# SwiGLU mixer of a two-layer diffusion trunk: plain block products for four tiles per half at both ends, norm by quarters, VectorE sums, stores issued by ScalarE

## The chip, the cores and the metric

The kernel runs on one core of a Trainium2 chip. The metric is the time of one execution on the device in microseconds (us), the median of several runs. The engines are named as in the profile: PE (TensorE, matmuls), PEld (its weight loads), DVE (VectorE), ACT (ScalarE), POOL (GpSimd), and SP, which only issues DMA. Each engine works its instructions in order, so a DMA that waits for its data holds up whatever stands behind it on the engine that issues it.

## The reference

One step of a trunk of two layers on 1152 tokens (1024 of a sample, 128 of a prompt) of width 1024, in fp32. `ada_mod` makes six modulation vectors per layer from `silu(c) @ w_ada` (1024 by 6144).

```python
for l in range(DEPTH):                      # l = 0: attention and retention, l = 1: gMLP
    h = modulate(rmsnorm(x, norm_g[l, 0]), sh1, sc1)
    y = ab(h) if l % 2 == 0 else chunk_gmlp(h)     # both end in an output projection
    x = x + g1 * y
    h = modulate(rmsnorm(x, norm_g[l, 1]), sh2, sc2)
    x = x + g2 * swiglu(h)
y = rmsnorm(x, final_norm_g)

def swiglu(h):                               # the mixer: d = 1024, D_FF = 2816
    return (silu(h @ w_gate) * (h @ w_up)) @ w_down
def chunk_gmlp(h):
    u, v = split(gelu(h @ w_in)); v = layernorm(v)
    v = einsum('gij,bnjgd->bnigd', w_s, chunks(v)) + b_s
    return (u * v) @ w_out
```

## The kernel before, in words

Tokens lie along the free axis, in two halves c = 0, 1 of 576, each of two pieces h = 0, 1 of 288; a quarter is one (c, h). X, the residual stream, lies in tiles x0 to x3 (`xp(f, c, h)` is one 128x288 block of it). An fp32 product is three matmuls on operands split in a high and a low part (hi by hi, hi by lo, lo by hi): ACT copies the high part, another engine subtracts it for the low one. That is the "prep" of an operand.

The **mixer** (`class Mixer`, `run`) works through `UNITS`, one unit for each 128 rows of D_FF (22 in all): the unit's gate and up products for one half or both. Then it does the `GROUPS` of down products. Both use seven block products in Strassen's manner in place of eight (`gate_up`, `down`, `steps`, `product`): 7 x 4 x 3 = 84 matmuls 128x288 for a unit and a half. Their seven left operands are built from the weight blocks by 4 sums, 7 copies and 7 subtractions 128x512 (`prep`), and their seven right operands (`RIGHT`, in tiles hq, h and x) from the normalised X. Units 20 and 21 are done for c = 0 alone at the start and for c = 1 alone at the end; the 20 others take both halves. After two units `combine` makes the seven right operands of the down product from their outputs (7 sums, 7 copies, 7 low parts, on DVE, POOL and ACT), and stores high and low part in DRAM (`hcd`). Before the downs `hload` brings them back, and X comes back from its spill `xtd`.

`proj_out` is the output projection ahead of a mixer: matmuls, `resid` adds into X, `squares` sums the squares, then `rnorm` scales a half of X, first c = 0, later c = 1, and builds the right operands, on DVE and POOL by turns. `xnorm` does the first norm of layer 1, behind the downs of layer 0. `last0`, `last1` and `done` take up the squares behind the last downs and finish.

Weights come as a **stream** `W` in program order: DMAs of 512 KB issued by SP into three slots of a staging tile ST, consumed by preps into rings w0 to w4. The ada weights of layer 1 are in that stream too, as 24 pairs of DMAs and 8 matmuls each (`in_w_ada`), one pair behind nearly every unit of mixer 0. Background generators (`bg`, `bg2`) fill the gaps; a planner decides only where in the program order their steps stand. All instructions are recorded by one helper, so that every row of the profile says L129.

## Time and profile before

| | |
|---|---|
| median of 3 runs | 2997.62 us (2991.59 to 2999.55) |
| profiled execution | 3002.7 us, its span 3000.9 us |
| PE busy | 2730.0 us (91%), 18667 matmuls |
| DVE, ACT, POOL busy | 1734.2, 1181.9, 1075.3 us |
| mean granted PE clock | 0.954 of full speed |

The span is the time from the first instruction to the last; the profiled execution took 1.8 us more than it. The stages are: attention layer to 825 us, output projection and entry of mixer 0 to 975, its units to about 1500, its end to 1600, its downs to 1725, then the hand-over to the gMLP layer, the gMLP layer to 2100, the entry of mixer 1 to 2225, its units to 2650, its end to 2775, downs and final norm to 3001.

### The profile page before, as it was taken

How to read it: one execution, taken by the hardware profiler on the slowest of the kernel's cores; microseconds unless marked ns; L12 is line 12 of the kernel's file. 1: busy time of each engine (PE TensorE's matmuls, PEld its weight loads, DVE VectorE, ACT ScalarE, POOL GpSimd, SP SyncE). 2: the span in 40 equal slices, each digit the busy share in tenths (PEclk: the TensorE clock that was granted, in tenths of full speed). 3: DMA queues.
4: the chain of work that ended last, by engine and by line, in shares of the span. 5: the costliest groups of instructions: out<-in, count | busy, mean ns of one | idle time of the engine just before them, and what ended most of it. 6: DMA issues, size and time to landing. Idle time of an engine off the chain costs nothing. (4 is left out here: it accounts for less than half of the span.)

```text
span 3000.9 us, 48879 instructions
## 1 busy us (share of the span) xinstructions
PE 2730.0 (91%) x18667; PEld 2570.7 (86%) x18667; DVE 1734.2 (58%) x3212; ACT 1181.9 (39%) x2385; POOL 1075.3 (36%) x978
## 2 busy tenths in 40 slices
PE   6999998998978899899789979999879999989996
PEld 5887897888977788888779977899879999988995
DVE  5651336877465444554577864534675555458875
ACT  5542225776344333333322244223554343342224
POOL 1120014665054232332366562000534334346553
PEclk8999998999988999899899999999989999999997
DMA  9385435332423554354598624124215344469761
GB/s 285 100 275 168 134 95 151 79 79 66 148 77 102 163 182 140 131 176 140 184 312 259 215 80 133 29 61 127 81 56 167 110 141 141 132 225 300 253 200 64
DMA packets 429344, 447.16 MB, mean 149 GB/s; under 512 B 25579, under 2 KB 368374, under 8 KB 427574
## 3 DMA queue, kind: packets, MB, share of 16 engines
q1 hardware_dynamic: 426704, 441.20, 46.3%
q8 instruction: 147, 2.41, 0.3%
q10 hardware_dynamic: 2406, 2.85, 0.3%
q14 instruction: 87, 0.71, 0.1%
HBM read 302.03 MB, written 141.93 MB: 148 GB/s over the span
## 5 line engine op out<-in xcount | busy, mean ns | idle before, releaser
L129 PE MATMUL PS<-hq,w 128*128 128x288 f32 (+1 forms) x10080 | 1521.7, 308 | 151.1 <-ACT SC L129 73.0
L129 PEld LDWEIGHTS PS<-hq,w 128*128 128x128 f32 x10080 | 1453.6, 194 | 186.3 <-ACT SC L129 86.0
L129 ACT CAST w<-ST 128x512 fp32r<-128x512 f32 (+3 forms) x733 | 377.5, 545 | 563.4 <-POOL ST L129 296.0
L129 DVE TENSOR_TENSOR w<-ST,w 128x512 fp32r<-128x512 f32 (+3 forms) x551 | 456.0, 849 | 240.5 <-ACT w L129 237.7
L129 DVE SCALAR_TENSOR_TENSOR x<-PS,mod,x 128x288 f32<-128x288 f32 (+2 forms) x944 | 388.4, 445 | 152.6 <-PE PS L129 147.0
L129 PE MATMUL PS<-h,w 128*128 128x288 f32 (+1 forms) x2702 | 418.9, 303 | 44.7 <-DVE x L129 25.0
L129 PEld LDWEIGHTS PS<-h,w 128*128 128x128 f32 (+1 forms) x2702 | 380.8, 192 | 74.3 <-DVE x L129 30.6
L129 POOL TENSOR_TENSOR SC<-SC 128x288 f32<-128x288 f32 (+2 forms) x122 | 116.9, 972 | 491.6 <-ACT SC L129 472.7
L129 PE MATMUL PS<-x,w 128*128 128x288 f32 (+1 forms) x1728 | 269.4, 304 | 12.8 <-ACT x L129 6.6
L129 PEld LDWEIGHTS PS<-x,w 128*128 128x128 f32 x1728 | 248.1, 192 | 19.5 <-ACT x L129 8.3
L129 ACT COPY SC<-PS 128x576 f32<-128x576 f32 (+8 forms) x249 | 128.6, 518 | 326.8 <-PE PS L129 304.7
L129 DVE TENSOR_TENSOR SC<-PS,SC 128x576 f32<-128x576 f32 (+3 forms) x131 | 90.3, 690 | 223.9 <-PE PS L129 216.1
L129 POOL TENSOR_TENSOR SC<-SC,x 128x576 fp32r<-128x576 f32 (+5 forms) x102 | 146.2, 1435 | 202.0 <-ACT x L129 129.1
L129 POOL TENSOR_TENSOR ST<-ST 128x256 f32<-128x256 f32 (+2 forms) x208 | 164.1, 789 | 150.2 <-DVE w L129 132.6
L129 DVE TENSOR_TENSOR ST<-ST 128x512 f32<-128x512 f32 x176 | 166.0, 943 | 2.1
L129 POOL TENSOR_TENSOR x<-x,SC 128x288 f32<-128x288 f32 (+2 forms) x21 | 25.6, 1234 | 358.2 <-ACT SC L129 335.0
L129 PE MATMUL PS<-w,hq 128*128 128x512 f32 x648 | 153.3, 395 | 0.0
L129 PEld LDWEIGHTS PS<-w,hq 128*128 128x128 f32 x648 | 120.9, 188 | 32.6 <-issue 4.7
L129 POOL TENSOR_TENSOR w<-ST,w 128x256 fp32r<-128x256 f32 (+1 forms) x182 | 128.5, 723 | 30.9 <-ACT w L129 25.0
L129 ACT ACTIVATE SC<-SC 128x576 f32<-128x576 f32 (+2 forms) x97 | 62.3, 643 | 170.6 <-DVE SC L129 170.5
L129 POOL TENSOR_TENSOR x<-x 128x576 fp32r<-128x576 f32 (+2 forms) x54 | 88.6, 1640 | 94.7 <-ACT x L129 60.5
L129 DVE TENSOR_TENSOR SC<-SC,PS 128x576 f32<-128x576 f32 (+3 forms) x60 | 40.2, 670 | 139.0 <-PE PS L129 122.7
(194 smaller groups left out, 2781.6 us busy)
## 6 DMA issues: line engine op xcount, KB each, us to landing
hq<-hcd SPq DMA_DIRECT2D x106, 576.0 KB, 8.8
hcd<-x SPq DMA_DIRECT2D x200, 288.0 KB, 2.8
ST<-in_w_ada SPq DMA_DIRECT2D x80, 512.0 KB, 4.8
h<-hcd SPq DMA_DIRECT2D x48, 576.0 KB, 8.4
ST<-in_w_ffn_gate SPq DMA_DIRECT2D x48, 512.0 KB, 5.3
ST<-in_w_ffn_up SPq DMA_DIRECT2D x48, 512.0 KB, 4.2
hcd<-SC SPq DMA_DIRECT2D x80, 288.0 KB, 3.6
ST<-in_w_ffn_down SPq DMA_DIRECT2D x80, 256.0 KB, 6.0
```

The lines of the kernel that those rows point to most:

```text
L129: return fn(*args, **kw)
```

## The change

- **Tiles.** Units 18 to 21 are done for c = 0 alone first and c = 1 alone last, by `plain`: eight block products on the weight blocks as they are, 96 matmuls, with a prep of 4 copies and 4 subtractions (`prep_plain`). In each mixer 8 unit-halves are so done, of which 4 were alone before too; the other 4 come out of units that took both halves.
- **Norm.** `rnorm` becomes `rscale(l, c, h)`, a quarter at a time as soon as its squares are there, and `rsplit(c, ...)`. All sums and low parts go on DVE. In `proj_out` the c = 1 groups run piece h = 0 for all eight f first, then h = 1, for which four weight units are fetched once more.
- **Combine.** All its sums and low parts are on DVE but for one combine, the last; its stores are issued by ACT, right behind the copies, in place of SP. In the whole program POOL has 408 instructions fewer, DVE 394 more, ACT 368 more (364 of them the stores).
- **Ada.** Of the 24 pairs of layer 1 eight stay in mixer 0, behind odd units; eight go between the pair units and eight between the column units of gMLP's input projection.
- **Hand-over.** The first four u units of gMLP for c = 0 stand ahead of the v tiles (`blockA` with `u_before`); X is spilled in `last0`.
- **Ends.** X and the first down operands are reloaded piece by piece during the last four units (`preload`, `hload`), where the planner sees a free DMA. The last group's downs for c = 1 alternate between two m (`down2`); the squares are taken by a generator queue of their own (`bg3`), and the last multiplications stand on DVE alone.

PE's program has 18080 matmuls in place of 17888 by the program's count of calls: 96 more in each mixer.

```diff
+    def rscale(l, c, h):
+        yield from rstd(c, (h,))
+        r = acc2(c)[:, HN * h:HN * h + HN]
+        for f in range(10):
+            if f < 8:
+                    x = xp(f, c, h)[:, s]
+                    V.scalar_tensor_tensor(x, x, A[:, f, cond:cond + 1], r[:, s], ALU.mult, ALU.mult)
+            if f > 1:
+                    x = xp(f - 2, c, h)[:, s]
+                    S.activation(x, x, AF.Identity, bias=B[:, f - 2, cond:cond + 1])
+            yield
+        scaled.add((c, h))
...
+    def rsplit(c, todo):
+        src = (b11, b21, b22, b11, b12, b22, b21)
+        diff = dict(T1=(b11, b12, b11), T3=(b12, b22, b12), T2=(b22, b22, b11), T4=(b21, b21, b22))
+        for z in todo:
+            for g in range(2):
+                if z in diff:
+                    V.tensor_tensor(*(a[g] for a in diff[z]), ALU.subtract)
+                    yield
+                    continue
+                op = int(z[1])
+                if z[0] == "C":
+                    if c and g == 0 and op in (2, 4, 6):
+                        RIGHT[op, c] = x_places(op // 2 - 1)
+                    S.copy(R(RIGHT[op, c][g][:, 0]), src[op][g])
+                else:
+                    hi, lo = (RIGHT[op, c][g][:, a] for a in range(2))
+                    V.tensor_tensor(R(lo), src[op][g], hi, ALU.subtract)
+                    if g:
+                        normed.add((op, c))
+                    yield
+    FIRST_Q = "C0 C1 L0 L1".split()
+    OTHER_Q = "T1 C5 C3 L5 T3 L3 T2 C2 C4 L2 L4 T4 C6 L6".split()
...
-    UNITS = [(20, (0,)), (21, (0,))] + [(u, (0, 1)) for u in range(20)] + [(20, (1,)), (21, (1,))]
+    UNITS = [(u, (0,)) for u in (20, 21, 18, 19)] + [(u, (0, 1)) for u in range(18)] + [(u, (1,)) for u in range(18, 22)]
...
-            if ada is not None and len(cs) == 2:
-                ada_next(1, ada, 2 if j in (1, 2, 3, 4) else 1)
+            if ada is not None and len(cs) == 2 and j % 2:
+                ada_next(1, ada)
...
-    ffn_stream(0, ada1_q)
+    ffn_stream(0, deque(ada1_q.popleft() for _ in range(8)))
     wc = ap["w_in_c"][0]
-    add_pairunits(wc, 1024)
-    add_pairunits(wc, 1536)
+    for m in range(4):
+        add_colunit(wc, 128 * m)
+    for q in range(2):
+        for u in range(4):
+            add_pairunit(wc, 1024 + 512 * q, u)
+            ada_next(1, ada1_q, 1)
...
-    for m in (*range(8), *range(4)):
+        ada_next(1, ada1_q, 1)
+    for m in (*range(8), *range(8)):
         add_colunit(ap["w_out_c"][0], 128 * m)
...
-                if bef and u == 0:
-                    bef(i)
-                group(u, 4 + u, i, rs[u])
+            group(u, 4 + u, 1, rs[u])
             W.release(rs[u])
+        rs = []
+        for i in (1, 3):
+            for u in range(4):
+                if i == 1:
+                    rs.append(W.take())
+                group(u, u, i, rs[u])
+                if i == 3:
+                    W.release(rs[u])
+            if i == 1:
+                bg_add(rscale(l, 1, 0))
         for u in range(4):
             r = W.take()
             if u == 3:
                 mix.begin()
-            for i in (1, 3):
-                group(u, u, i, r)
+            group(u, 4 + u, 3, r)
             W.release(r)
-        nr[1] = bg_add(rnorm(l, 1, normed))
+        bg_add(rscale(l, 1, 1))
+        rplaces(1)
+        for z in (FIRST_Q, OTHER_Q):
+            bg_add(rsplit(1, z))
...
+            its = [W.block() for _ in range(2)]
+            O = self.left[key] = []
+            for it in its:
+                for s in range(2):
+                    while not self.avail():
+                        yield self.avail
+                    O.append((self.slot(), None))
+                    v = it["v"][:, 4 * s:4 * s + 4]
+                    hi, lo = (O[-1][0][0][:, a].rearrange("p (f n) -> p f n", n=P) for a in range(2))
+                    S.copy(R(hi), v)
+                    V.tensor_tensor(R(lo), v, hi, ALU.subtract)
+                    yield
+                W.free(it)
...
+        def plain(self, key, c, su, t0, t1, before=None, after=None):
+            turn, self.pt = self.pt, self.pt + 4
+            def b(j):
+                j = (turn + j) % 6
+                return PS[:, j:j + 1, :HN]
+            for n, (j, i, op) in enumerate(((0, 0, 0), (1, 2, 0), (2, 0, 3), (3, 2, 3), (0, 1, 1), (1, 3, 1), (2, 1, 5), (3, 3, 5))):
+                if before:
+                    before(op)
+                s = self.left[key][i][0]
+                fill([s[0][:, :, 0:P], RIGHT[op, c][0]])
+                for k in range(4):
+                    z = RIGHT[op, c][k // 2][:, :, k % 2]
+                    for a, h in ((0, 0), (0, 1), (1, 0)):
+                        TE.matmul(b(j)[:, 0], lhsT=R(s[0][:, a, P * k:P * k + P]), rhs=R(z[:, h]),
+                                  start=(k, a, h) == (0, 0, 0) and n < 4, stop=(k, a) == (3, 1), skip_group_check=True)
+                if n == 0:
+                    S.copy(t1, b(0))
...
+                    V.tensor_tensor(t1, su, t1, ALU.mult)
+                if n in (2, 3, 6, 7):
+                    self.put(s)
+                next(self.gen, None)
+                if after:
+                    after(n)
+                tick()
...
+        def combine(self, p, cs, a0, a1, b0, b1, t, h0, h1, e=V, G=V):
 
             g, f = (0, 0) if p == 0 else (1 + (p - 1) // 2, (p - 1) % 2)
 
-            def out(op, hi, lo):
-                for a, v in enumerate((hi, lo)):
-                    d = hcd[g, op][:, a, f, HN * cs[0]:HN * cs[-1] + HN]
-                    SY.dma_start(out=d.rearrange("p (c n) -> p c n", n=HN), in_=v)
-            sent = []
-            def low(op, x, h, e=G):
+            def send(op, a, v):
+                d = hcd[g, op][:, a, f, HN * cs[0]:HN * cs[-1] + HN]
+                S.dma_start(out=d.rearrange("p (c n) -> p c n", n=HN), in_=v)
+            def high(op, h, x):
+                S.copy(R(h), x)
+                send(op, 0, h)
...
+        def down2(self, g, m0, c):
+            def right(i, k, c):
+                return self.right[g, i, c][0][:, :, k]
+            for i in range(7):
+                for j in range(2):
+                    m = m0 + j
+                    b = 2 * self.BANKS[i] + j
+                    self.product(i, (g, m), GROUPS[g][1], right, (c,), b)
+                    self.put(self.left[g, m][i][0])
+                    f, h = ((m, 0), (m, 0), (m, 1), (m + 4, 1), (m + 4, 1), (m, 1), (m + 4, 0))[i]
+                    x = xp(f, c, h)
+                    for cond, s in psegs(c, h):
+                        V.scalar_tensor_tensor(x[:, s], PS[:, b, s], mcol(self.l, 5, f, cond), x[:, s], ALU.mult, ALU.add)
+                    tick()
...
+                        if clk.t["D"] < clk.t["T"] + 3.0:
+                            if xq and (u > 18 or i > 3):
+                                preload(*xq.popleft())
+                            else:
+                                self.hload(2)
+                    self.plain(k, 1, one(sc(1728)), *t[u], after=free1)
+                    if u != 20:
+                        endcomb()
+                    while xq and u == 21:
+                        preload(*xq.popleft())
...
-            for m in range(4):
-                self.down(5, m, (1,))
+            ahead[0] = 1.5
+            for m in (0, 2):
+                self.down2(5, m, 1)
                 last(1, m)
...
+    def u_before(ci):
+        while hn[0] <= ci:
+            bg_step()
+    blockA(4, ev_u(0), before=u_before, chunks=PAIRED[:2])
...
-        g = bg_add(gen())
-        if c:
-            drain(g)
+        for f in (m, m + 4):
+            for h in range(2):
+                x = xp(f, c, h)
+                bg3.append(squares(c, h, f, lambda x=x, f=f: S.activation(x, x, AF.Copy, scale=P2[:, 19 + f:20 + f])))
```

Three places in the instruction order. First SP, the DMAs it issues in the middle of mixer 0 (ST is the staging tile, hcd the DRAM scratch). Before:

```order
L129 DMA ST_65<-in_w_ffn_up 128x8x128
L129 DMA ST_65<-in_w_ada 128x1024
L129 DMA hcd_86<-x3_78_6104 128x576 x2
L129 DMA ST_65<-in_w_ada 128x1024
L129 DMA ST_65<-in_w_ffn_gate 128x8x128
L129 DMA hcd_86<-x3_78_6104 128x576 x3
L129 DMA hcd_86<-SC_66 128x576
L129 DMA hcd_86<-x3_78_6104 128x576
L129 DMA hcd_86<-SC_66 128x576
```

Of the change, the same stretch of two units:

```order
L129 DMA ST_65<-in_w_ffn_up 128x8x128
L129 DMA ST_65<-in_w_ffn_gate 128x8x128
L129 DMA ST_65<-in_w_ffn_up 128x8x128
L129 DMA ST_65<-in_w_ada 128x1024 x2
L129 DMA ST_65<-in_w_ffn_gate 128x8x128
L129 DMA ST_65<-in_w_ffn_up 128x8x128
L129 DMA ST_65<-in_w_ffn_gate 128x8x128
L129 DMA ST_65<-in_w_ffn_up 128x8x128
```

The stores to hcd have left SP, and the ada pair stands behind every second unit, both of its loads next to each other. What ACT issues in the change (end of mixer 0, where the tiles are 288 wide):

```order
L129 ACTIVATE SC_66<-PS_74 128x288
L129 DMA hcd_86<-SC_66 128x288
L129 CAST SC_66<-SC_66 128x288
L129 DMA hcd_86<-SC_66 128x288
L129 CAST SC_66<-SC_66 128x288
L129 DMA hcd_86<-SC_66 128x288
L129 ACTIVATE SC_66<-SC_66 128x288
L129 DMA hcd_86<-SC_66 128x288 x2
L129 CAST SC_66<-SC_66 128x288
L129 DMA hcd_86<-SC_66 128x288
```

Each copy or activation that makes a high part is followed by its store, and the stores of low parts stand between.

Second PE, where the last downs of mixer 0 (h and hq as right operands, 128x288) meet gMLP. The moving operand is named first. Before, the v tiles (128x512, a ring moving) follow at once, with the norm's sums of c = 1 (ones, SC) among them:

```order
L129 MATMUL PS_74<-hq0_13_219,hq2_19_465 128x288 x6
L129 MATMUL PS_74<-hq0_13_219,hq3_20_535 128x288 x6
L129 MATMUL PS_74<-hq1_17_331,hq2_19_465 128x288 x6
L129 MATMUL PS_74<-w4_101_15008,hq0_13_219 128x512 x6
L129 MATMUL PS_74<-w2_102_15012,hq1_17_331 128x512 x6
L129 MATMUL PS_74<-w1_103_15016,hq2_19_465 128x512 x6
L129 MATMUL PS_74<-w4_101_15008,hq0_13_219 128x512 x6
L129 MATMUL PS_74<-w2_102_15012,hq1_17_331 128x512 x6
L129 MATMUL PS_74<-w1_103_15016,hq2_19_465 128x512 x6
L129 MATMUL PS_74<-ones_88,SC_66 96x2 x6
L129 MATMUL PS_74<-w0_104_15051,hq3_20_535 128x512 x12
L129 MATMUL PS_74<-SC_66,ones_88 128x288
```

In the change the down rows are followed by 32 rows of u units (hq moving, 128x288), then the v tiles; here is the end of that stretch:

```order
L129 MATMUL PS_74<-hq3_20_535,w1_107_14902 128x288 x6
L129 MATMUL PS_74<-ST_65,S32_92 32x512 x4
L129 MATMUL PS_74<-SC_66,ones_88 128x288
L129 MATMUL PS_74<-hq0_13_219,w2_111_15092 128x288 x6
L129 MATMUL PS_74<-hq1_17_331,w2_111_15092 128x288 x6
L129 MATMUL PS_74<-SC_66,ones_88 128x288
L129 MATMUL PS_74<-hq2_19_465,w2_111_15092 128x288 x6
L129 MATMUL PS_74<-hq3_20_535,w2_111_15092 128x288 x6
L129 MATMUL PS_74<-ST_65,S32_92 32x512 x4
L129 MATMUL PS_74<-w0_112_15096,hq0_13_219 128x512 x6
L129 MATMUL PS_74<-w3_113_15224,hq1_17_331 128x512 x6
L129 MATMUL PS_74<-w4_114_15293,hq2_19_465 128x512 x6
```

The ada products (ST, S32) stand among the u units and v tiles, and the norm of c = 1 beside u units.

Third the entry of mixer 1, where c = 0 is split into right operands while PE runs the output projection for c = 1 (evictions x3<-PS). Before, DVE:

```order
L129 TENSOR_TENSOR x0_97_11970<-x0_97_11970 128x2x288
L129 SCALAR_TENSOR_TENSOR x1_98_11995<-x1_98_11995,acol11_98,SC_66 128x288 x2
L129 TENSOR_TENSOR hq3_20_535<-x0_97_11970,hq3_20_535 128x2x288
L129 SCALAR_TENSOR_TENSOR x3_100_12081<-PS_74,mod1_94,x3_100_12081 128x288
L129 TENSOR_TENSOR w0_133_17470<-ST_65,w0_133_17470 128x1024
L129 TENSOR_TENSOR h1_131_17333<-x1_98_11995,h1_131_17333 128x576
L129 TENSOR_TENSOR x0_97_11970<-x1_98_11995,x0_97_11970 128x2x288
L129 TENSOR_TENSOR x1_98_11995<-x1_98_11995,x0_97_11970 128x2x288
L129 TENSOR_TENSOR h0_130_17332<-x0_97_11970,h0_130_17332 128x576
L129 TENSOR_TENSOR hq2_19_465<-x1_98_11995,hq2_19_465 128x2x288
```

and beside it POOL:

```order
L129 TENSOR_TENSOR x0_97_11970<-x0_97_11970 128x2x288
L129 TENSOR_TENSOR x1_98_11995<-x1_98_11995,SC_66 128x288
L129 TENSOR_TENSOR hq3_20_535<-x0_97_11970,hq3_20_535 128x2x288
L129 TENSOR_TENSOR h1_131_17333<-x1_98_11995,h1_131_17333 128x576
L129 TENSOR_TENSOR x0_97_11970<-x1_98_11995,x0_97_11970 128x2x288
L129 TENSOR_TENSOR x1_98_11995<-x1_98_11995,x0_97_11970 128x2x288
L129 TENSOR_TENSOR hq2_19_465<-x1_98_11995,hq2_19_465 128x2x288
L129 TENSOR_TENSOR h0_130_17332<-x0_97_11970,h0_130_17332 128x576
L129 TENSOR_TENSOR x1_98_11995<-x1_98_11995 128x2x288
```

In the change, on DVE alone:

```order
L129 SCALAR_TENSOR_TENSOR x1_102_11573<-x1_102_11573,acol11_98,SC_66 128x288 x4
L129 TENSOR_TENSOR hq0_13_219<-x0_101_11572,hq0_13_219 128x2x288 x2
L129 TENSOR_TENSOR hq1_17_331<-x1_102_11573,hq1_17_331 128x2x288 x2
L129 TENSOR_TENSOR x0_101_11572<-x0_101_11572 128x2x288 x2
L129 TENSOR_TENSOR h1_139_17473<-x1_102_11573,h1_139_17473 128x576 x2
L129 TENSOR_TENSOR x0_101_11572<-x1_102_11573,x0_101_11572 128x2x288 x2
L129 TENSOR_TENSOR hq3_20_535<-x0_101_11572,hq3_20_535 128x2x288 x2
L129 TENSOR_TENSOR x1_102_11573<-x1_102_11573,x0_101_11572 128x2x288 x2
L129 TENSOR_TENSOR hq2_19_465<-x1_102_11573,hq2_19_465 128x2x288 x2
L129 TENSOR_TENSOR h0_138_17472<-x0_101_11572,h0_138_17472 128x576 x2
L129 TENSOR_TENSOR x1_102_11573<-x1_102_11573 128x2x288 x2
L129 TENSOR_TENSOR h2_140_17474<-x1_102_11573,h2_140_17474 128x576 x2
L129 SCALAR_TENSOR_TENSOR x3_104_11716<-PS_74,mod1_94,x3_104_11716 128x288
L129 TENSOR_TENSOR w2_142_17618<-ST_65,w2_142_17618 128x1024
```

The rows that POOL had are in DVE's queue now, one behind the other, and the preparation of the next projection weights (w2 here) stands behind all of them, where before such a row (w0) stood in the middle.

## Rows read from the trace of the kernel before

**Rows 1.** the page's busy times by engine, share of the span, instructions.

```profile
PE 2730.0 (91%) x18667; PEld 2570.7 (86%) x18667; DVE 1734.2 (58%) x3212; ACT 1181.9 (39%) x2385; POOL 1075.3 (36%) x978
```

**Rows 2.** busy us (instructions) per engine by stage; clock, DMA share, GB/s.

```profile
825.00:975.00 150.00, 117.48 (x761) 109.09 (x760) 89.75 (x123) 68.93 (x132) 73.60 (x59) 0.86 0.29 90
975.00:1100.00 125.00, 109.54 (x756) 100.05 (x754) 54.93 (x71) 39.37 (x64) 33.47 (x23) 0.95 0.49 159
1100.00:1475.00 375.00, 340.76 (x2375) 322.89 (x2376) 188.86 (x219) 127.85 (x210) 119.17 (x74) 0.93 0.47 155
1475.00:1600.00 125.00, 104.21 (x704) 97.42 (x703) 92.32 (x198) 38.13 (x101) 73.13 (x96) 0.95 0.84 274
1600.00:1725.00 125.00, 125.00 (x945) 125.00 (x944) 101.66 (x237) 29.70 (x82) 70.41 (x93) 1.00 0.76 243
...
2100.00:2225.00 125.00, 92.70 (x615) 89.40 (x614) 87.72 (x123) 67.15 (x129) 63.43 (x47) 0.86 0.19 58
...
2275.00:2650.00 375.00, 366.44 (x2739) 364.61 (x2738) 197.69 (x257) 148.37 (x252) 138.58 (x89) 1.00 0.41 137
2650.00:2775.00 125.00, 113.23 (x790) 107.70 (x790) 88.45 (x203) 39.91 (x105) 72.27 (x98) 0.97 0.85 275
...
2900.00:2990.00 90.00, 70.88 (x442) 65.27 (x440) 57.57 (x127) 40.71 (x94) 36.65 (x45) 0.88 0.22 72
```

**Rows 3.** PE's timeline in mixer 0, 1195 to 1225 (S is ada's).

```profile
1211.72 9.44 PE L129 MATMUL PS<-hq,w 128*128 128x288 f32 x48 [3.60 <-ACT SC L129]
1221.10 1.06 PE L129 MATMUL PS<-ST,S 128*32 128x512 f32 x8
```

**Rows 4.** windows restricted to tile S, the ada products.

```profile
975.00:1475.00 500.00, 22.37 (x168) 3.32 (x168) 0.00 (x0) 0.00 (x0) 0.94 0.47 156
1100.00:1475.00 375.00, 14.92 (x112) 2.21 (x112) 0.00 (x0) 0.00 (x0) 0.93 0.47 155
```

**Rows 5.** what PE waited for, 1100 to 1475: us, times, longest.

```profile
PE PS L129 <- ACT SC L129: 34.2, 13, 3.6
```

**Rows 6.** what SP's queue waited for, 1100 to 1475.

```profile
SPq L129 <- ACT x L129: 103.2, 14, 13.5
```

**Rows 7.** SP's timeline, 1190 to 1240: start, us, DMA issued.

```profile
1206.23 2.25 SPq L129 DMA_DIRECT2D hcd<-x  x2
1212.95 0.33 SPq L129 DMA_DIRECT2D ST<-in_w_ada  x1
```

**Rows 8.** what ACT waited for, 1100 to 1475.

```profile
ACT x L129 <- DMA hcd<-x: 35.4, 27, 3.9
```

**Rows 9.** the timeline of all engines, 2170 to 2216, first mixer-1 products.

```profile
2207.59 3.83 DVE L129 TENSOR_TENSOR x<-x,x 128x576 f32<-128x576 f32 x2
2208.89 3.79 POOL L129 TENSOR_TENSOR x<-x,x 128x576 f32<-128x576 f32 x2
```

**Rows 10.** DVE's groups by form, 2275 to 2650: busy, mean ns, idle before.

```profile
L129 DVE TENSOR_TENSOR w<-ST,w 128x512 fp32r<-128x512 f32 x112 | 96.8, 899 | 0.0
...
L129 DVE TENSOR_TENSOR x<-x 128x576 fp32r<-128x576 f32 x8 | 6.0, 751 | 0.0
```

**Rows 11.** what PE waited for, 2100 to 2225.

```profile
PE PS L129 <- ACT hq L129: 12.4, 1, 12.4
PE PS L129 <- DVE x L129: 9.7, 4, 9.0
```

**Rows 12.** what PE waited for, 1725 to 1825.

```profile
PE PS L129 <- DVE x L129: 22.9, 6, 14.0
```

**Rows 13.** the timeline of all engines, 2976 to 3001, the end.

```profile
2982.11 0.44 ACT L129 ACTIVATE SC<-x 128x288 f32<-128x288 f32 x1 [2.75 <-DVE x L129]
...
2982.59 0.54 ACT L129 ACTIVATE x<-x,P 128x288 f32<-128x288 f32 x1
```

**Rows 14.** POOL's groups by form, 1100 to 1475.

```profile
L129 POOL TENSOR_TENSOR x<-SC 128x576 f32<-128x576 f32 x14 | 20.9, 1494 | 30.1 <-ACT SC L129 26.9 <-DMA hcd<-x 3.1
```

**Rows 15.** the page's DMA issues: KB each, us to landing.

```profile
hcd<-x SPq DMA_DIRECT2D x200, 288.0 KB, 2.8
```

More of the change, by code (lines that the diff above doesn't have):

```diff
@@ L364, in fill @@
             moved = False
-            for q in (bg2, bg):
+            for q in (bg3, bg2, bg):
                 now = max(clk.t["T"], clk.ready(aps))
-                if not q or max(clk.t["V"], clk.t["S"], clk.t["G"] - 1.0) > now + AHEAD:
+                if not q or max(clk.t["V"], clk.t["S"], clk.t["G"] - 1.0) > now + ahead[0]:
                     continue
@@ L500, in rstd, with squares @@
-    def rstd(c):
-        a, rc = acc2(c), rs96[:, c]
-        yield [a]
+    count = {}
+    def squares(c, h, f, then=None, eng=V):
+        acc, n = acc2(c)[:, HN * h:HN * h + HN], count.get((c, h), 0)
+        count[c, h] = n + 1
+        if n == 0:
+            S.activation(acc, xp(f, c, h), AF.Square)
+            if then:
+                then()
+        else:
+            sqi[0] ^= 1
+            q = SC[:, 3072 + HN * sqi[0]:3072 + HN * sqi[0] + HN]
+            S.activation(q, xp(f, c, h), AF.Square)
+            if then:
+                then()
+            yield
+            eng.tensor_tensor(acc, acc, q, ALU.add)
+        yield
@@ L1918, in prep, with prep_plain @@
             lo()
-            for i in its:
-                W.free(i)
+            W.free(its[0])
+        def prep_plain(self, key):
+            while not W.loaded(2):
+                yield lambda: W.loaded(2)
+            its = [W.block() for _ in range(2)]
[9 more added lines that the diff above has]
+                    V.tensor_tensor(R(lo), v, hi, ALU.subtract)
+                    yield
+                W.free(it)
         def begin(self):
-            self.gen = self.prep(0, 4, G, [V] * 7)
+            self.gen = self.prep_plain(0)
             bg2.append(self.gen)
@@ L2033, in combine @@
+            low(b1, h1)
             yield
[L2034 removed]
+            send(5, 1, b1)
+            high(1, h0, b0)
+            yield
             G.tensor_tensor(t, b0, a0, ALU.subtract)
[L2036 to L2037 removed]
+            low(b0, h0)
+            high(2, h1, a0)
             yield
[L2039 to L2041 removed]
+            send(1, 1, b0)
+            low(a0, h1)
             yield
[L2043 to L2044 removed]
+            send(2, 1, a0)
@@ L2180, in run @@
-                    self.gate_up(k, cs, *Z3, Z3[0], Z3[2], after=free1)
-                    late = self.combine(10, cs, *t[0], Z3[0], Z3[2], *(one(sc(1152 * (i < 2) + HN * i)) for i in range(3)), G)
+                        if u == 18 and i == 0:
+                            for q in range(3):
+                                XT[q] = newx(q)
+                        if u == 19 and i == 0:
+                            XT[3] = newx(3)
+                            xq.extend((1, 1, h) for h in range(2))
@@ L2182, in run @@
+                    while xq and u == 21:
+                        preload(*xq.popleft())
+                    if u == 19 or u == 21:
+                        late = self.combine(u // 2, cs, *t[u - 1], *t[u], *(one(sc(o)) for o in (1152, 1440, 2016)), V if u == 19 else G, V if u == 19 else G)
+                        comb[0] = late if u == 19 else iter(())
             for g in range(6):
@@ L2220, in run @@
             bank_i[0] = 6
+            ahead[0] = AHEAD
             done(1)
```

295 lines of the change are left out of this document (128 added, 167 removed).

## The prediction

> **What bounds the kernel now.** I read the busy times first: PE is busy for 91% of the span, the next engine for 58% [rows 1]. So the question is where PE's other 9% lies, and the part of its busy time that isn't work. For that I cut the span into stages [rows 2] and take one stage as the measure: from 1600 to 1725 PE is never idle, at a clock of 1.00, and does 945 matmuls in 125.00 us, 0.132 us each. A stage's loss is its length less its matmuls times 0.132, which counts idle time and low clock alike:
>
> - entry of mixer 0: 150 - 761 x 0.1323 = 49 us; entry of mixer 1: 125 - 615 x 0.1323 = 44 us;
> - end of mixer 0's units: 125 - 704 x 0.1323 = 32 us; of mixer 1's: 125 - 790 x 0.1323 = 20 us;
> - hand-over: its matmuls are of mixed sizes, so I take PE's waits for X, 22.9 us [rows 12];
> - middle of mixer 1's units: 375 - 2739 x 0.1323 = 13 us; the end from 2900: 31 us, then 11 us without PE.
>
> The middle of mixer 0 has other work in it, the ada products. Two units with both halves are 336 matmuls, so a pair of units takes 375 / (2739 / 336) = 46.0 us in mixer 1. In mixer 0, with its 112 ada matmuls taken off (14 pairs of 8 matmuls; from 975 on 168, 21 pairs [rows 4]), it takes 375 / ((2375 - 112) / 336) = 55.7 us. That is 6.73 pairs of units, 14 ada pairs: (375 - 6.73 x 46.0) / 14 = 4.7 us for an ada pair; from 975 to 1100 the same sum gives 29 / 7 = 4.2. With 4.5 each the 21 pairs cost 94 us, while their own matmuls are busy for 22.37 us in all [rows 4], 1.07 each. The rest is seen in the timeline: PE waits 3.60 us for an operand and the next 48 matmuls take 9.44 us, 0.197 each, before the ada matmuls come [rows 3]. Such waits are 13 in 375 us [rows 5], and the granted clock of the stage is 0.93 against 1.00 in mixer 1 [rows 2]. What is late is the weights: SP stood for 103.2 us waiting for ACT's copies [rows 6], since its store of a copy stands ahead of the next loads; in the timeline the store at 1206.23 is let go late and the second ada load follows at 1212.95 [rows 7].
>
> **The change, part by part.**
>
> *Plain tiles.* 192 matmuls more, 192 x 0.1323 = **+25.4 us**, certain as long as PE is the bound. For it four units with one half stand at each end, 4 x 96 x 0.1323 = 50.8 us of PE work, where two stood with 2 x 84 x 0.1323 = 22.2 us. That is the cover for the next parts.
>
> *Entries.* PE waited 12.4 us for a high part in hq and 9.7 us for X there [rows 11]. Just ahead of such a wait DVE and POOL each do two subtractions 128x576 side by side and take 3.83 and 3.79 us for two [rows 9], 1.9 each, where DVE alone needs 0.75 [rows 10]. Two engines in parallel so do 1.05 a microsecond, DVE by itself 1.33. By the Trainium skill ("SBUF — State Buffer", section "SBUF: two separate sides") a VectorE operation with two inputs in SBUF and a GpSimd one exclude each other for a whole instruction. The trace agrees, 3.8 against 1.5 us for two, so by that page giving POOL's share to VectorE loses nothing.
> After the change a quarter has 8 scalings of about 0.5 us and a half 22 subtractions of 0.75: 4 + 16.5 = 20.6 us on DVE behind the last square of c = 1. The plain units cover it with 50.8 us. But DVE has more to do in these: four preps (16 subtractions 128x512, 0.62 each by the fastest of them, 10 us), 5.5 for the units' own sums, 13 for two combines of half width, 7.5 for the next Strassen prep: some 57 us in 50.8, all estimates from 0.75 us a tile of 576. So a few microseconds stay. For c = 0 the burst of 16.5 us stands ahead of the next projection weights in DVE's queue, as the order shows; behind it waits PE's next column unit, which the units in the rings cover for all but some 6 us. Together a remainder of 15 to 20 us of 44 to 49. I take 27 and 26 = **-53 us**; bounds: nothing, if the wait is only moved to the weights, and 80, if 6 us remain at each entry.
>
> *Ada and stores.* Sixteen of 24 pairs leave mixer 0 and save 16 x 4.5 = 72 us there. In gMLP a pair costs 1.07 us at least and 4.5 if the waits go along. I take 2.0, near its own, since there no combine stores stand in SP's queue and the DMA share of that stage is below that of the mixers: 16 x (4.5 - 2.0) = **-40 us**. Bounds: 0, and 72 (all 21 counted at their own 22.4 of 94). The eight that stay could get cheaper too, since the stores leave SP: that is in the upper bound, not in the sum. The move of the stores costs ACT 364 issues. SP needed 0.33 us for one issue [rows 7], so 6 us a pair of units by 14 stores x 0.4, on an engine that is busy for 148 of 375 us [rows 2]: hidden, and what then stands behind a store on ACT is an eviction; without slack there it would cost at most those 6 us x 17. The Trainium skill ("DMA: Bandwidth & Descriptors", section "Issuing engines are not separate DMA queues") has it that another issuing engine saves only the sequencer's time for the issue, usually little. By that the move of the stores alone would give nothing; the trace shows the queue waiting 103.2 us for data, not for issues. My sum takes no gain for the stores by themselves.
>
> *Ends of the units.* X and the first down operands came in at the end, with a DMA share of 0.84 and 0.85 in those stages [rows 2]. They now start within 50.8 us of plain work, piece by piece. Of 32 and 20 us I take 20 and 11 = **-31 us**; bounds 5 and 46, for the transfers take the same bandwidth, only earlier.
>
> *Hand-over.* Of the 22.9 us the longest wait was 14.0 [rows 12]: the norm of a half behind the last downs. Four u units of c = 0 are 4 x 2 x 24 x 0.1323 = 25 us of work that needs that norm as well, by quarters, but no c = 1. I take **-16**; bounds 5 and 23.
>
> *Middle of the units.* POOL's 89 instructions in 375 us become some 67 us on DVE at 0.75, so 198 + 67 = 265 of 375: 71%, and DVE's own get shorter (w<-ST at 899 ns, [rows 10]). **-2** for both mixers; bounds +15 and -10.
>
> *End.* Two m alternate, so an add into X has a second product beside it: of the 31 us some 11 go. Against it, squares and scalings stand on ACT in a row behind the last add, 0.44 + 0.54 us a pair [rows 13], some 6 pairs more. **-5**; bounds +5 and -15.
>
> Sum: 25.4 - 53 - 40 - 31 - 16 - 2 - 5 = -121.6. The profiled execution took 3002.7 us: 2881; it stands 5.1 us above the median of the runs shown, so the forecast is **2876 us**.
>
> **The rivals.**
>
> *Ada costs the same everywhere* (+40): the wait is tied to the pair, two loads of 512 KB through three slots and eight matmuls, not to mixer 0. For it: 4.2 and 4.7 us in both parts of mixer 0. Against: there the store queue is what SP waits for. 2916 us.
>
> *The bursts hold the weights up* (+53): the norm in DVE's queue is in front of projection and plain preps, and PE waits for DVE w in place of DVE x. For it: the 57 us in 50.8 and the 16.5 us burst. Against: quarters start early. 2929 us.
>
> *All hides* (-45): ada pairs at their own price (16 x 0.9 = 15) and entries and ends near their bounds (30 more). 2831 us.
>
> *Slower: DVE waits for stores.* A tile that has been stored is overwritten by the next subtraction in the same combine. A store needs 2.8 us to land [rows 15]; POOL waited 3.1 us for that in 14 sums [rows 14], ACT 35.4 in 27 waits [rows 8]. POOL had time; on DVE every wait holds up preps and evictions behind it, and so PE. Three full waits in each of 18 combines, 3 x 3.6 x 18 = 194 us: 3070 us. It decides from 122 / 18 = 6.8 us a combine on. Against: two or three preps stand between store and overwriting, and the 3.1 us on POOL.
>
> *Nothing is covered:* the waits have other causes, and only 25 us are added, with a few gained: 3000 to 3025.
>
> **How the numbers follow.** Forecast 0.50 (2850 to 2905); ada 0.16; bursts 0.14; all hides 0.12; stores 0.05; nothing covered 0.03. A measurement of this kernel can tell about 0.3%, 9 us, from no change. Range 2820 to 2945: it takes in forecast, ada, bursts and most of "all hides". Faster 0.91, same 0.02, slower 0.07.
>
> **What would show it.** PE's matmuls 128x288 up by 192; a pair of units in the middle of mixer 0 near 50.5 us with one ada pair in two units (46 + 4.5) or near 47 if that gets cheap; SP no longer waiting for ACT x; POOL idle in the units, DVE's w<-ST down from 899 ns; loss at the two entries under 25 us each, with DVE w as what is waited for; in gMLP the clock staying near 1.00 in spite of 16 ada pairs. Wrong would make it: waits of DVE for hcd in the middle of the units; gMLP longer by over 60 us (before it took 375, from 1725 to 2100); PE waiting for DMA there.

## The result, and the profile after

The changed kernel takes 2858.12 us (median of 4 runs, 2852.79 to 2861.21) against 2997.52 us (4 runs): the ratio is 0.9536, with a 95% interval of 0.9516 to 0.9557, so 139 us less. 2876 us were forecast, range 2820 to 2945. The profiled execution of the change took 2860.08 us, its span 2858.0 us, 142.9 us below that of before. One execution of the run with the sums on VectorE in the kernel before took 13363 us and is left out of its ratio.

The page's busy times by engine answer to [rows 1]:

```profile
PE 2702.6 (95%) x18859; PEld 2552.9 (89%) x18859; DVE 1789.8 (63%) x3606; ACT 1168.2 (41%) x2389; POOL 514.3 (18%) x570
```

PE has the 192 matmuls more that were counted, and is still busy for 27 us less: its mean granted clock is 0.975 against 0.954. POOL has lost half its time, 561 us, and DVE has gained only 56.

The stages, busy us (instructions) of PE, PEld, DVE, ACT, POOL, then clock, DMA share and GB/s, answer to [rows 2]; each stage now lies earlier in the span:

```profile
800.00:975.00 175.00, 165.22 (x1200) 161.92 (x1199) 128.68 (x239) 90.44 (x180) 0.00 (x0) 0.97 0.39 118
975.00:1350.00 375.00, 371.11 (x2785) 362.96 (x2784) 223.41 (x339) 145.53 (x246) 0.00 (x0) 1.00 0.53 176
1350.00:1450.00 100.00, 93.88 (x660) 89.58 (x659) 73.48 (x180) 33.63 (x93) 45.47 (x74) 0.98 0.75 240
1600.00:1725.00 125.00, 112.75 (x697) 97.18 (x697) 84.50 (x198) 56.11 (x120) 15.22 (x19) 0.97 0.39 131
1725.00:1975.00 250.00, 239.82 (x1549) 209.67 (x1548) 113.10 (x311) 70.39 (x128) 0.00 (x0) 0.99 0.39 120
1975.00:2100.00 125.00, 109.49 (x783) 107.69 (x782) 91.61 (x178) 67.09 (x136) 0.00 (x0) 0.93 0.34 103
2100.00:2525.00 425.00, 420.82 (x3155) 419.65 (x3154) 262.75 (x403) 170.87 (x291) 0.00 (x0) 1.00 0.46 155
2525.00:2600.00 75.00, 70.05 (x479) 65.77 (x478) 52.85 (x133) 25.22 (x71) 27.67 (x50) 0.98 0.84 269
2750.00:2858.00 108.00, 77.86 (x524) 74.88 (x522) 76.47 (x170) 42.90 (x101) 27.48 (x36) 0.85 0.26 87
```

Loss is again length less matmuls times 0.1323 us. The entry of mixer 0 loses 175 - 1200 x 0.1323 = 16 us (49 before), that of mixer 1 125 - 783 x 0.1323 = 21 us (44), the ends of the units 13 and 12 us (32 and 20). The middle of mixer 1 loses 425 - 3155 x 0.1323 = 8 us (13 in a shorter stretch). The largest step is the middle of mixer 0. With the ada matmuls taken off, it lost 500 - (756 + 2375 - 168) x 0.1323 = 108 us with 21 pairs; now 375 - (2785 - 56) x 0.1323 = 14 us with 7. The pairs are counted by the windows on tile S:

```profile
975.00:1350.00 375.00, 7.46 (x56) 1.10 (x56) 0.00 (x0) 0.00 (x0) 1.00 0.53 176
1725.00:1975.00 250.00, 14.88 (x88) 2.21 (x88) 0.00 (x0) 0.00 (x0) 0.99 0.39 120
```

So a pair costs 14 / 7 = 2.0 us at most in the mixer. The same sum gives 108 / 21 = 5.1 before; the 4.5 of the prediction has the loss taken off that units have without ada. All prices of a pair below are by the sum that takes nothing off. PE waits there for 3.9 us in all, against 34.2 [rows 5]:

```profile
PE PS L129 <- DVE SC L129: 3.9, 3, 1.9
```

In gMLP, from 1725 to 1975, PE is idle for 10.2 us and busy with 11 pairs for 14.9. At the hand-over it waited for DVE 9.1 us, against 22.9 [rows 12]; at the entry of mixer 1 a single wait is left, and at the end the norm's sums wait for the squares. The waits of PE from 1600 to 1725, from 1975 to 2100 and from 2750 on:

```profile
PE PS L129 <- DVE x L129: 9.1, 8, 2.5
```

```profile
PE PS L129 <- ACT w L129: 9.5, 1, 9.5
```

```profile
PE PS L129 <- DVE SC L129: 11.7, 2, 10.3
```

### The profile page after: what moved, and what is told of

It is laid out like the page before. It is cut to its first block, busy times and chain, and to the rows that moved or that the text cites. A ratio compares the mean times of both kernels' runs of the same rounds, so it can differ in the third digit from the quotient of the medians.

```text
span 2858.0 us, 49003 instructions
## 1 busy us (share of the span) xinstructions
PE 2702.6 (95%) x18859; PEld 2552.9 (89%) x18859; DVE 1789.8 (63%) x3606; ACT 1168.2 (41%) x2389; POOL 514.3 (18%) x570
## 4 chain that ended last, share of the span: by engine, by line
PE 70%; DVE 10%; DMA 5%; ACT 4%; issue 3%; POOL 1%; ACTq 0%; SPq 0%; DVEq 0%; POOLq 0%
PE PS L129 70%; DVE x L129 4%; DVE SC L129 2%; DVE w L129 2%; DMA hcd<-SC 2%; ACT x L129 1%; ACT w L129 1%; ACT SC L129 1%; DVE hq L129 1%; DMA ST<-in_w_ada 1%; POOL ST L129 1%; DMA w<-krd 0%; DMA rgd<-SC 0%; DMA w<-knd 0%; DMA ST<-in_w_in_c 0%
## 5 line engine op out<-in xcount | busy, mean ns | idle before, releaser
L129 DVE TENSOR_TENSOR w<-ST,w 128x512 fp32r<-128x512 f32 (+3 forms) x539 | 384.2, 730 | 292.6 <-ACT w L129 288.0
L129 PE MATMUL PS<-x,w 128*128 128x288 f32 (+1 forms) x1440 | 219.9, 300 | 3.0 <-ACT adac L129 2.0
L129 PEld LDWEIGHTS PS<-x,w 128*128 128x128 f32 x1440 | 204.4, 189 | 4.9 <-ACT h L129 2.4
L129 POOL TENSOR_TENSOR ST<-ST 128x256 f32<-128x256 f32 (+1 forms) x192 | 140.4, 731 | 151.5 <-DVE w L129 134.7
L129 DVE TENSOR_TENSOR SC<-SC 128x288 f32<-128x288 f32 (+5 forms) x215 | 104.9, 496 | 63.4 <-ACT SC L129 47.4
L129 PE MATMUL PS<-w,w 96*128 96x512 f32 x384 | 109.6, 421 | 6.2 <-DMA w<-krd 2.7
L129 DVE TENSOR_TENSOR SC<-SC,x 128x576 fp32r<-128x576 f32 (+1 forms) x90 | 68.1, 757 | 68.4 <-DMA hcd<-SC 50.0
L129 DVE TENSOR_REDUCE sm<-PS 128x1 f32<-128x1152 f32 (+1 forms) x72 | 89.1, 1237 | 25.7 <-PE PS L129 25.0
L129 ACT ACTIVATE SC<-x 128x288 f32<-128x288 f32 x128 | 55.2, 440 | 118.1 <-DVE x L129 95.6
L129 DVE TENSOR_TENSOR ST<-ST 128x512 f32<-128x512 f32 x144 | 98.9, 687 | 1.8
```

Of the source, the lines that this page charges most:

```text
L129: return fn(*args, **kw)
```

## The experiments

All ratios are to the kernel before; differences in us are ratio times 2998. Two theories were held against each other at first, for the largest step: A, that the stores in SP's queue made an ada pair cost 4.5 us; B, that the pair's own loads did.

**Stores alone, in the kernel before.**

```diff
-                    SY.dma_start(out=d.rearrange("p (c n) -> p c n", n=HN), in_=v)
+                    S.dma_start(out=d.rearrange("p (c n) -> p c n", n=HN), in_=v)
```

> The kernel before with one edit: combine's stores to hcd are issued by ACT instead of SP. Theory A (the stores in SP's queue, waiting for ACT's copies, hold the weight loads back, and that is what makes an ada pair cost 4.5 us): the middle of mixer 0 loses some 25 us instead of 109, so the time falls by 60 to 85 us, to 2915 to 2940 us; SP no longer waits for ACT x. Theory B (the cost is the pair's own: two loads of 512 KB through three slots and 8 matmuls): the stores' place changes nothing in mixer 0, 2990 to 3005 us. ACT's issues, some 14 x 0.4 us in a pair of units, could also cost a few us in mixer 1.

Measured: 1.003 (1.0015 to 1.0044), 9 us slower. Theory A falls. What PE waited for from 1100 to 1475 is as before (34.2 us [rows 5]):

```profile
PE PS L129 <- ACT SC L129: 36.8, 14, 3.6
```

SP's waits show where the stores' wait went. What SP waited for, 1100 to 1475, in the kernel before beside the 103.2 us for ACT's copies [rows 6]:

```profile
SPq L129 <- DVE w L129: 99.7, 14, 10.1
```

and in this run:

```profile
SPq L129 <- DVE w L129: 214.9, 14, 19.2
SPq L129 <- PE PS L129: 100.0, 13, 9.4
```

99.7 + 103.2 = 203 us before, 215 here: the wait for stores has turned into a longer wait for DVE w, which is the prep that gives a staging slot back. So SP seems to have waited in front of a store for something that came no later than the slot it needed next.

**Ada pairs alone, in the kernel before.** The edit is the change's own (`ffn_stream` and gMLP's stream).

> The kernel before with one edit: 16 of the 24 ada pairs are moved from mixer 0 to the gMLP layer, as in the change (8 behind pair units, 8 behind column units); stores stay on SP. Theory A: mixer 0 gains 16 x 4.5 = 72 us, gMLP loses 16 x 1.1 to 2.2 = 18 to 35 us, so 2945 to 2960 us. Theory B (a pair costs the same wherever it stands): 2990 to 3005 us.

Measured: 0.9889 (0.9866 to 0.9911), 33 us faster, between the ranges of both theories. If each of the 16 pairs saved 4.5 us, 39 of the 72 us are paid again, 2.4 us a pair in gMLP; that split is an estimate and not read from a trace. The run tells what moving a pair is worth in that kernel, 2.1 us, not why.

**Ada pairs put back, in the change.**

```diff
+            if ada is not None and len(cs) == 2:
+                ada_next(1, ada, 2 if j in (1, 2, 3, 4, 5, 6) else 1)
...
+    ffn_stream(0, ada1_q)
```

> The changed kernel with one edit: all 24 ada pairs are back in mixer 0 (two behind units 1 to 6, one behind each other one with both halves), none in gMLP; stores stay on ACT. Theory A: with the stores gone from SP a pair costs little more than its own 1.07 us in mixer 0, so 16 pairs add 17 to 25 us there, and gMLP gets back the some 35 us that it lost: 2840 to 2860 us, no slower than the change. Theory B: 16 x 4.5 = 72 us more in mixer 0, 35 back: 2880 to 2900 us.

Measured: 0.9513 (0.9491 to 0.9536), level with the change. Windows of this run, all of the program and then tile S:

```profile
975.00:1350.00 375.00, 365.67 (x2684) 343.74 (x2683) 220.27 (x336) 140.71 (x237) 0.00 (x0) 0.99 0.56 186
1725.00:1975.00 250.00, 249.33 (x1591) 230.27 (x1590) 126.32 (x353) 81.47 (x157) 0.00 (x0) 1.00 0.26 76
```

```profile
975.00:1350.00 375.00, 21.98 (x152) 3.44 (x152) 0.00 (x0) 0.00 (x0) 0.99 0.56 186
```

In mixer 0, 375 - (2684 - 152) x 0.1323 = 40 us for 19 pairs, 2.1 each at most; in gMLP PE's idle time falls from 10.2 to 0.7 us and 14.9 us of ada work go, 24 us for 11 pairs, 2.2 each. In the changed kernel a pair costs the same at both places, and moving it is worth nothing.

**Stores put back on SP, in the change.** The reverse of the first edit.

> The changed kernel with one edit: combine's stores are issued by SP again, at the same places in the program. Theory A: the eight ada pairs that are left in mixer 0 cost 3 to 4 us more each, 25 to 35 us, and units without ada a little: 2880 to 2910 us, with SP waiting for ACT or DVE ahead of the stores. Theory B: 2850 to 2866 us, as the change.

Measured: 0.9517 (0.9492 to 0.9543), level with the change. With these four, the pair is cheap in the change for a reason that is neither its place nor the stores. Two other edits are left. One is part of the change, though the list ahead of the prediction lacks it: `product` steps the prep of the next unit between the two halves too, 14 steps a unit in place of 7, and `prep` gives its first staging slot back as soon as it has been read. The other is the move of the sums off POOL.

**Early prep alone, in the kernel before.**

```diff
             for c in cs:
+                if c != cs[0] and nk == 4:
+                    next(self.gen, None)
...
             add.tensor_tensor(a12, a12, a11, ALU.subtract)
+            if nf == 4:
+                W.free(its[1])
```

> The kernel before with one edit: the next unit's prep is stepped after each half of a block product (14 steps a unit, not 7), and the first of its two staging slots is given back as soon as it has been read. Theory C (stepping: the prep of a unit is spread over the whole unit before, so the slots come free late and an ada pair, which takes two more, makes the next weights late): ada pairs fall from 4.5 us to 1 to 2 us each, 50 to 70 us less, 2930 to 2955 us. Theory D (the sums on POOL slow DVE's preps by sharing a port, and that makes them late): 2990 to 3005 us.

Measured: 0.9795 (0.9769 to 0.982), 61 us faster, as theory C expected. Windows 1000 to 1400, all and tile S, of the kernel before and of this run:

```profile
1000.00:1400.00 400.00, 360.58 (x2508) 338.33 (x2507) 197.42 (x233) 134.05 (x220) 123.66 (x78) 0.94 0.47 157
1000.00:1400.00 400.00, 18.11 (x136) 2.69 (x136) 0.00 (x0) 0.00 (x0) 0.94 0.47 157
```

```profile
1000.00:1400.00 400.00, 388.38 (x2875) 366.09 (x2874) 211.79 (x265) 146.49 (x248) 138.93 (x89) 1.00 0.53 175
```

```profile
1000.00:1400.00 400.00, 21.70 (x152) 3.29 (x152) 0.00 (x0) 0.00 (x0) 1.00 0.53 175
```

400 - (2875 - 152) x 0.1323 = 40 us for 19 pairs: 2.1 each, as in the change, with the stores on SP and the sums on POOL. Before it was 400 - (2508 - 136) x 0.1323 = 86 us for 17 pairs, 5.1 each.

The trace of the kernel before shows the chain that is shortened. Four of its rows, from 1100 to 1112:

```profile
1100.44 1.88 DVE L129 TENSOR_TENSOR ST<-ST 128x512 f32<-128x512 f32 x1
1102.35 0.62 ACT L129 CAST w<-ST 128x512 fp32r<-128x512 f32 x1 [3.56 <-DVE ST L129]
1102.88 0.63 ACT L129 COPY SC<-PS 128x576 f32<-128x576 f32 x1
1103.57 8.53 PE L129 MATMUL PS<-hq,w 128*128 128x288 f32 x48 [3.61 <-ACT SC L129]
```

PE waits for ACT to copy a finished product out of PS, the tile that matmuls write (SC<-PS). That eviction stands on ACT behind a weight copy (w<-ST), and the copy waits 3.56 us for a sum of the prep on DVE (ST<-ST). All 13 waits of [rows 5] end so, with an eviction right behind a copy that had waited for such a sum. It isn't the weight that PE waits for. What ACT's copies waited for, 1000 to 1400, in the kernel before and in this run, and PE's wait in this run (34.1 us before):

```profile
ACT w L129 <- DVE ST L129: 77.2, 35, 4.2
```

```profile
ACT w L129 <- DVE ST L129: 18.9, 18, 1.8
PE PS L129 <- ACT SC L129: 10.1, 8, 2.1
```

ACT's waits for the loads themselves hardly fell (59.5 and 56.7 us in all). SP still waits long for the preps that free its slots:

```profile
SPq L129 <- DVE w L129: 79.2, 17, 6.7
```

Which of the two parts does it, the finer steps or the earlier slot, was not tried.

**Late prep, in the change.** The reverse edit.

> The changed kernel with the reverse edit: the prep is stepped once a block product (7 steps a unit), slots given back at its end. Theory C: the eight pairs in mixer 0 cost 3.4 us more each and the two-unit periods some more: 2885 to 2900 us. Theory D: 2850 to 2866 us, as the change.

Measured: 0.9592 (0.9572 to 0.9612), 17 us slower than the change, intervals apart, and still below the range of theory C. From 975 to 1350 the loss is 375 - (2699 - 56) x 0.1323 = 25 us against 14, so the seven pairs there cost at most 1.6 us more each and not 3.4. Theory C holds in both directions, in the change at half the size.

```profile
975.00:1350.00 375.00, 363.93 (x2699) 353.50 (x2699) 220.52 (x337) 143.26 (x242) 0.00 (x0) 1.00 0.50 169
```

**Sums of combine on VectorE alone, in the kernel before.** `G` is V in `combine`, and in the last multiplication of `gate_up`.

> The kernel before with one edit: all sums and low parts of combine, and the last multiplication of gate_up, on VectorE instead of POOL. Theory D: DVE's prep groups fall from 951 and 1145 ns to 730 and 700 ns, ada pairs get cheap: 2925 to 2950 us. Theory C: the preps still come late, 2985 to 3005 us.

Measured: 0.9895 (0.987 to 0.992), 31 us faster, between the ranges of both theories: D is right too, and smaller than it expected. DVE's groups by form, 1100 to 1475, in the kernel before and in this run:

```profile
L129 DVE TENSOR_TENSOR w<-ST,w 128x512 fp32r<-128x512 f32 x94 | 86.4, 951 | 8.8 <-ACT w L129 8.0
L129 DVE TENSOR_TENSOR ST<-ST 128x512 f32<-128x512 f32 x53 | 60.7, 1145 | 0.4
```

```profile
L129 DVE TENSOR_TENSOR w<-ST,w 128x512 fp32r<-128x512 f32 x104 | 68.3, 686 | 19.8 <-ACT w L129 18.6
L129 DVE TENSOR_TENSOR ST<-ST 128x512 f32<-128x512 f32 x60 | 42.4, 707 | 0.6
```

Means of 686 and 707 ns are reached with POOL silent; with POOL at work the first was 899 even in mixer 1 [rows 10]. The sum in the chain above is one of the second group: it took 1.88 us with POOL at work beside it. ACT's copies wait 56.8 us for these sums in this run, 77.5 before, and PE for ACT's evictions 25.9 us, 34.2 before.

**Sums of combine on POOL, in the change.**

> The changed kernel with the reverse edit: combine's sums and low parts (but those of operands 1 and 4) and the last multiplication of gate_up on POOL, as before. Theory D: eight ada pairs cost 3.4 us more each, and contention returns: 2885 to 2910 us. Theory C: 2850 to 2870 us.

Measured: 0.9758 (0.9733 to 0.9783), 67 us slower than the change, more than theory D expected: the dearest edit to undo. DVE's group by form, DVE's waits and PE's, 975 to 1350:

```profile
L129 DVE TENSOR_TENSOR w<-ST,w 128x512 fp32r<-128x512 f32 x103 | 100.4, 992 | 60.2 <-ACT w L129 60.2
```

```profile
DVE SC L129 <- POOL SC L129: 41.5, 8, 6.3
```

```profile
PE PS L129 <- DVE SC L129: 24.5, 8, 4.2
```

The prep takes 992 ns in place of 687 in the change (row below), and there is a second cost, which no theory had: the low part that stands on DVE waits up to 6.3 us for POOL's sum, and with it, in DVE's order, the eviction that PE waits for next, eight times for 24.5 us in all.

```profile
L129 DVE TENSOR_TENSOR w<-ST,w 128x512 fp32r<-128x512 f32 x108 | 71.8, 687 | 45.0 <-ACT w L129 45.0
L129 DVE TENSOR_TENSOR ST<-ST 128x512 f32<-128x512 f32 x56 | 38.5, 687 | 0.7
```

It isn't a matter of the ada pairs. Mixer 1 has none, and there 375 us lose 375 - 2617 x 0.1323 = 29 us, where the change loses 8 in 425:

```profile
2150.00:2525.00 375.00, 354.52 (x2617) 352.89 (x2616) 204.14 (x249) 145.49 (x245) 135.81 (x86) 0.98 0.39 129
```

**Two plain tiles per half in place of four, in the change.**

```diff
-    UNITS = [(u, (0,)) for u in (20, 21, 18, 19)] + [(u, (0, 1)) for u in range(18)] + [(u, (1,)) for u in range(18, 22)]
+    UNITS = [(u, (0,)) for u in (20, 21)] + [(u, (0, 1)) for u in range(20)] + [(u, (1,)) for u in (20, 21)]
```

> The changed kernel with two plain tiles per half at each end in place of four (units 20 and 21; 18 and 19 take both halves by seven products again), 96 matmuls fewer, 12.7 us of PE work. Theory E (the four plain units are needed as cover for the norm of c = 1 at the entries and for the reloads at the ends): 25 us of cover are gone at each of four places, 10 us or more come back at each entry and 5 or more at each end: 2870 to 2900 us. Theory F (quarters and VectorE's sums have already made the entries short, two are enough): 2843 to 2850 us.

Measured: 0.9615 (0.9601 to 0.9629), 24 us slower than the change with 96 matmuls (12.7 us) fewer. Windows at the two entries and ends (entry 0, end 0, entry 1, end 1):

```profile
800.00:975.00 175.00, 157.38 (x1120) 153.08 (x1119) 123.31 (x222) 84.28 (x161) 0.00 (x0) 0.94 0.39 119
1375.00:1475.00 100.00, 92.59 (x633) 88.48 (x632) 76.96 (x195) 29.00 (x86) 60.06 (x93) 0.95 0.84 270
2000.00:2125.00 125.00, 104.12 (x724) 102.67 (x724) 90.34 (x170) 63.79 (x125) 0.00 (x0) 0.89 0.27 82
2550.00:2650.00 100.00, 91.17 (x626) 86.59 (x625) 71.30 (x172) 31.48 (x85) 46.34 (x75) 0.97 0.81 263
```

Losses are 27, 16, 29 and 17 us where the change has 16, 13, 21 and 12: 27 us come back at these four places and 12.7 go with the matmuls; some 10 us more come from stages that weren't separated.

**Half of the splits on POOL, in the change.** `(G if g else V)` in `rsplit`, but for the low parts of operands 0 and 1.

> The changed kernel with one edit: in rsplit the second tile of each sum, and of the low parts of operands 2 to 6, on POOL, as before, beside VectorE. Theory E (two engines on one port do less than VectorE alone): each entry gets 3 to 10 us longer, 2864 to 2880 us. Theory F (who does the splits doesn't matter, the quarters do): 2852 to 2864 us.

Measured: 0.9567 (0.9551 to 0.9583), 9 us slower than the change, with intervals that overlap by a little, so the time alone doesn't show it. In the trace, which is of the slowest of its four executions, the entry of mixer 1 loses 125 - 737 x 0.1323 = 28 us against 21, and PE's wait for a weight copy is 14.6 us in place of 9.5:

```profile
1975.00:2100.00 125.00, 102.97 (x737) 101.53 (x737) 89.43 (x148) 61.71 (x127) 32.11 (x18) 0.90 0.26 79
```

```profile
PE PS L129 <- ACT w L129: 14.6, 1, 14.6
```

**The v tiles first, in the change.** `blockA(4, ..., PAIRED[:2])` and its four weight loads are taken out, c = 0's u units stand with c = 1's.

> The changed kernel with one edit: the first four u units of gMLP for c = 0 stand behind the v tiles again, with c = 1's, and their four weight units aren't loaded twice. Theory E (they fill the wait for the norm at the hand-over): 10 to 20 us longer, 2868 to 2880 us. Theory F (the wait only moves): 2850 to 2864 us.

Measured: 0.9545 (0.953 to 0.9559), level with the change. PE's waits, 1600 to 1725:

```profile
PE PS L129 <- DVE x L129: 8.1, 7, 2.5
```

The hand-over stays short without the u units. What shortened it is another part of the change; which, was not tried.

**Weights ahead of the splits, 18 ada pairs in mixer 0, in the change.**

```diff
-        for z in (FIRST_Q, OTHER_Q):
-            bg_add(rsplit(0, z))
+        bg_add(rsplit(0, FIRST_Q))
...
             W.release(rs[u])
+            W.pump(force=True)
+        rs = [W.take() for _ in range(4)]
+        bg_add(rsplit(0, OTHER_Q))
```

> The changed kernel with two edits whose effects lie in different stages. First: in the output projection for c = 1, the next weight unit is prepared as soon as a ring is released, and the long part of c = 0's splits (OTHER_Q) is queued only behind these preps; in the trace of the change PE waited 9.5 us at once there, at the entry of mixer 1, for a weight copy that stood behind the splits on ACT. If that is the cause, that wait is gone and the entry of mixer 1 loses 10 to 14 us in place of 23; if the weights come late by their loads, it stays. Second: 18 ada pairs in mixer 0, one behind each unit with both halves, 6 behind column units of gMLP. If a pair costs about 1.4 us in the mixer and 2 in gMLP, mixer 0's middle loses about 28 us in place of 16 and gMLP 10 to 14 in place of 31. In all 2835 to 2848 us; if neither holds, 2852 to 2864.

Measured: 0.9545 (0.953 to 0.9561), level with the change. The wait for the weight copy is gone, as expected, but another stands in its place, PE's waits from 1970 to 2100 and the two rows of its timeline around it:

```profile
PE PS L129 <- DVE SC L129: 14.4, 1, 14.4
```

```profile
1995.82 1.23 PE L129 MATMUL PS<-hq,w 128*128 128x288 f32 x8
2011.49 1.12 PE L129 MATMUL PS<-ones,SC 128*96 128x2 f32 x6 [14.45 <-DVE SC L129]
```

Those six matmuls sum the squares of the next quarter (ones by SC). DVE's adds into X and its sums of squares for that quarter now stand among the splits. Weights, splits and squares share the queues of DVE and ACT, and what comes last there is what PE waits for. The second edit moves a cost and saves none: the 15 pairs from 975 to 1350 cost 375 - (2780 - 120) x 0.1323 = 23 us, 9 more than the seven of the change, and gMLP gets 9 us back. No version was found that beats the change beyond its interval.

## Why the prediction was right, step by step

139 us less were measured and 122 forecast. Part of that is luck: most steps came out at their size, but the saving of the largest came from edits other than the two it was put down to. Added up from the stages above, the steps give 25 - 55 - 58 - 28 - 14 - 7 - 3 = -140 us, an estimate, in the order of the list below.

- **Plain tiles, +25.4 us.** Right: 18859 - 18667 = 192 matmuls, and the two-tile run shows that the second half of them saves 24 us more than it costs.
- **Entries, -53 us.** Measured 33 and 22 us, 55 together. The mechanism holds in three parts: the cover (two tiles: +11 and +8 us), VectorE alone (splits on POOL: +9 us, not clear of noise), and the remainder. That remainder was put at "some 6 us" for a column unit whose weights stand behind the splits; it is the 9.5 us above, and what PE waits for is ACT's weight copy (ACT w), where DVE w was named as the sign. The granted clock of that stage is 0.93, against 0.86 before and 1.00 in the units behind it.
- **Ada and stores, -40 us.** This is the step that failed, in cause and in size. A price of 4.5 us in mixer 0 agrees with 5.1 less the units' own loss, and 2.0 in gMLP is near the measured 2.2. But I took the price as one of the place, with the stores in SP's queue as its reason: "What is late is the weights: SP stood for 103.2 us waiting for ACT's copies". [rows 5] named what PE waited for, ACT SC, and I passed over it: an eviction on ACT behind a weight copy that waits for a sum of the prep. The early prep alone brings a pair from 5.1 to 2.1 us where it stands, and is worth 61 us; it stands in no term of the sum. The stores are worth nothing, in either kernel. Mixer 0's middle gained 108 - 14 = 94 us where 72 were counted, and gMLP pays 25 us for 11 pairs, so some 36 for 16: -58 in place of -40. Moving the pairs is no longer a part of it: put back, the time is the same. A pair of units takes 375 / (2729 / 336) = 46.2 us with its share of ada, where 50.5 was the forecast and 47 the sign of pairs that get cheap.
- **Ends, -31 us.** Measured 19 and 9 us, 28 together. With two tiles 4 and 6 us come back, so the cover is a part of it and not all; the other parts were not tried one by one.
- **Hand-over, -16 us.** Waits fell by 22.9 - 9.1 = 13.8 us, so the size was right by luck; the reason given, the u units, was not: without them the wait is 8.1 us.
- **Middle of the units, -2 us.** Mixer 1's middle lost 13 us in 375 and loses 8 in 425, so -7 there. By itself the term is mis-sized, and the most telling: I counted that POOL's work fits on DVE (71% busy) and took next to nothing for the contention that goes. The sums on DVE are worth 31 us in the kernel before and 67 in the change; part of that stands in the 58 above.
- **End, -5 us.** Loss from 2750 on is 108 - 524 x 0.1323 = 39 us, against 31 + 11 before: -3. The squares in a row on ACT are the 10.3 us wait above, as feared.

The terms overlap, since the prep's steps, the length of its sums and the number of pairs bear on the same chain. Alone, early prep, sums on DVE and fewer pairs give 61 + 31 + 33 = 125 us in the kernel before, and undone one by one in the change 17, 67 and none.

Of the rivals, "ada costs the same everywhere" was right in what it says (2.1 and 2.2 us) and wrong in its price, for all of it had become cheap. The slower one, that DVE waits for stores, is there, as its sign said, but it costs little. DVE's waits for hcd, 975 to 1350 in the change:

```profile
DVE SC L129 <- DMA hcd<-SC: 24.7, 9, 3.8
DVE x L129 <- DMA hcd<-x: 14.3, 8, 2.7
```

That is 39 us in some 8 pairs of units, 4.8 us a pair, and not far from the 6.8 us at which it was to decide. It lies in time that DVE has to spare: PE waited 3.9 us in the same stretch. By the Trainium skill ("DMA: Bandwidth & Descriptors", section "Issuing engines are not separate DMA queues") another issuing engine saves only the time of the issue, which is usually small beside the DMA. By that the stores' move should give little; the runs agree, +0.003 alone and -0.002 undone, both about the size of an interval. By the same skill ("SBUF — State Buffer", section "SBUF: two separate sides") a VectorE operation with two operands in SBUF and a GpSimd one that reads SBUF block each other for a whole instruction. 687 against 992 ns for the same prep agrees.
